# Hybrid mLSTM and windowed-attention layer: TensorE in a fixed order through the attention, value products of two steps together, gate chain and v weights placed anew

## The chip, the cores and the metric

The kernel runs on one core of one Trainium2 chip. The metric is the time of one execution on the device, in microseconds (us). TensorE (PE in the profile) multiplies matrices into PSUM, VectorE (DVE) and ScalarE (ACT) evacuate PSUM and do the elementwise work, GpSimd (POOL) does elementwise work between SBUF tiles, and SyncE (SP) issues the DMAs. Each engine works through its own queue in order, and semaphores join them.

## The reference

One layer of a bidirectional encoder on 1024 tokens of width 1024, in float32. A single input projection feeds two groups of heads:

- four mLSTM heads of width 128: q and k go through a centred convolution of five taps and a SiLU; input and forget gates give a chunkwise recurrence with a matrix state, once forward and once backward; the two directions are added, normalised per head and gated by a sigmoid of the projection o;
- eight attention heads of width 64 with two key/value heads: each block of 128 queries sees its own block of keys and the two beside it, with a distance penalty and a sink logit per head.

Both results go through the output projection, then `x <- LN(alpha*x + mix)`, then a SwiGLU FFN of inner width 2816 with a gated per-layer input, and a second layer norm.

```python
s = jnp.einsum('bnqhgd,bnkhd->bnhgqk', qb, kb) * (A_HEAD_DIM ** -0.5)
s = jnp.where(valid[:, None, None], s + bias, -jnp.inf)
mx = jnp.maximum(s.max(-1, keepdims=True), sk)
e = jnp.exp(s - mx)
prob = e / (e.sum(-1, keepdims=True) + jnp.exp(sk - mx))
out = jnp.einsum('bnhgqk,bnkhd->bnqhgd', prob, vb)
```

## The kernel before, in words

**Precision.** Most matrices are kept as a pair: a rounded high part and the low rest (`split`, L90: ScalarE casts the high part, POOL or DVE subtracts). `mm3` (L111) multiplies two such pairs with three products, high by high, high by low, low by high; one call of it over a contraction of 128 is what the text calls a projection unit, with a moving operand of 512 columns. Transposes, value products and the mLSTM products are plain float32; a float32 product is two records in the trace.

**Order.** The program is traced in the order in which the code is written, and a planner then orders each engine's queue: it simulates the engines and takes, at each moment, the ready instruction that was traced first. Long projections are "fillers" (L119 to L174): generators that yield after each unit. `fill(n)` (L125) traces the next n units at a lower priority, so that they go where TensorE has nothing better; `until(name)` forces a tile to be finished. The planner may set any instruction earlier or later than its place in the text as long as its data allow it.

**Stages of the core.**

1. *First projection* (L293 to L315): attention keys and values and the gates of all 1024 tokens, eight PSUM banks c0ps; ScalarE copies the keys to akn (L314), DVE copies the values to av and adds the gate biases.
2. *Keys* (L324 to L335): per half of the tokens four transposes into one bank, 128 columns of two key heads each; then each head's 64 rows are copied to both the upper and the lower 64 partitions of k2, high part on ScalarE and low part on DVE.
3. *Gate chain* (L337 to L412): the prelude (L343 to L349) makes log-sigmoids on DVE and ScalarE; then TensorE transposes (gt), DVE scans (L359 to L363), two small products (gmp, mcp), and a last set of transposes (gcp) that DVE copies to gcol. Two results go to DRAM (mwd) for later.
4. *v weights* (L420 to L424): four loads of 512 KB on SP into the two-buffered raw tile, which the aq and qk weights also use, each split into vuh (ScalarE) and vul (POOL).
5. *Attention* (L501 to L514): 32 steps (four pairs of heads by eight query blocks). Step i traces `scores` (L446: four products, then softmax on DVE and ScalarE, last scaled by POOL at L467), then `transposed` of step i - 2 (L470: four or six transposes; ScalarE evacuates the first half of eT, DVE the second), then `weighted` of step i - 3 (L484: value products, each with 64 columns of the array, into one bank per four steps). Between them stand `fill(1)`, `fill(3)` and `fill(1)` (RA, L29). The fillers there are the aq tiles (queries), the eight v tiles and the first two qk tiles, 160 units in the loop.
6. *mLSTM heads* (L544 to L638): per head transposes of k, state products `up` (L568) in six groups, score products, numerators `nd` (L607, L609), normalisation of hs (L625), and for the head before it `gated` (L628): transposes tr of hs, multiplied into the sigmoid of o. Fillers: qk tiles 2 to 7, o tiles, and the attention part of the output projection. A qk tile ends in five passes of convolution over 1024 columns on DVE (L282, L284).
7. Output projection, first layer norm, FFN with Winograd-style sums, second layer norm; the change does not touch them.

Of the kernel before, what the change touches and what calls it, by code (L numbers as in the profile page):

```python
# [7 lines left out]
F32 = mybir.dt.float32  # L8
# [20 lines left out]
RA = (1, 3, 1)  # L29
# [6 lines left out]
def hybrid_layer(  # L36
# [7 lines left out]
    pe, act, dve, pool = nc.tensor, nc.scalar, nc.vector, nc.gpsimd  # L44
# [54 lines left out]
    def load_w(src, shape, name, eng_lo=None, raw=None):  # L99
        if raw is None:  # L100
            raw = wp.tile([P] + shape, F32, name="raw_" + name, tag="raw", bufs=2)
        nc.sync.dma_start(raw, src)
        hi = wp.tile([P] + shape, F32R, name="hi_" + name, tag="whi", bufs=4)
        lo = wp.tile([P] + shape, F32R, name="lo_" + name, tag="wlo", bufs=4)
        f = flat if len(shape) == 2 else (lambda t: t)
        split(f(hi), f(lo), f(raw), eng_lo)
        return hi, lo
# [200 lines left out]
    akn = [Y([P, 4, P], F32, f"akn{i}") for i in range(2)]  # L308
    GI = W([P, 2, MH, NT], F32, "GI")
    GF = W([P, 2, MH, NT], F32, "GF")  # L310
    for t in range(NT):
        dve.tensor_tensor(GI.rearrange("p d h c -> p (d h) c")[:, :, t], c0ps[t][:, 256:264], bg[:, 0:8], ALU.add)
        dve.tensor_tensor(GF.rearrange("p d h c -> p (d h) c")[:, :, t], c0ps[t][:, 264:272], bg[:, 8:16], ALU.add)
        act.copy(akn[t // 4][:, t % 4, :], c0ps[t][:, 0:128])  # L314
        dve.tensor_copy(av[:, t, :], c0ps[t][:, 128:256])  # L315

# [7 lines left out]
    for hf in range(2):  # L324
        akT = bank(f"akT{hf}", "sp")
        for t in range(4):
            pe.transpose(akT[:, t * P:(t + 1) * P], akn[hf][:, t, :], ident)
        cs = slice(hf * 512, hf * 512 + 512)
        for kv in range(2):
            src = akT[kv * 64:kv * 64 + 64, :]  # L330
            h, l = k2[kv]
            act.copy(h[0:64, cs], src)
            act.copy(h[64:128, cs], src)
            dve.tensor_tensor(l[0:64, cs], src, h[0:64, cs].bitcast(F32), ALU.subtract)
            dve.tensor_tensor(l[64:128, cs], src, h[64:128, cs].bitcast(F32), ALU.subtract)  # L335
# [14 lines left out]
    gt = bank("gt", "et")  # L350
    pe.transpose(gt[:G64, 0:P], g3, ident)
    pe.transpose(gt[:G64, P:2 * P], gi, ident)
    lfI = gA[:G64, 192:448].rearrange("p (a b) -> p a b", b=P)
    dve.tensor_copy(lfI.rearrange("p a b -> p (a b)"), gt[:G64, 0:2 * P])
    bt = gA[:G64, 448:576]
    Ar = gA[:G64, 576:704]
    Mr = gA[:G64, 704:832]
    gm = gA[:G64, 832:834]
    dve.tensor_tensor_scan(bt[0:32, :], ones[0:32, :], lfI[0:32, 0, :], 0.0, ALU.mult, ALU.add)  # L359
    dve.tensor_tensor_scan(bt[32:64, ::-1], ones[32:64, :], lfI[32:64, 0, ::-1], 0.0, ALU.mult, ALU.add)  # L360
    dve.tensor_tensor(Ar, lfI[:, 1, :], bt, ALU.subtract)
    dve.tensor_tensor_scan(Mr[0:32, :], Ar[0:32, :], Ar[0:32, :], -BIG, ALU.max, ALU.max)
    dve.tensor_tensor_scan(Mr[32:64, ::-1], Ar[32:64, ::-1], Ar[32:64, ::-1], -BIG, ALU.max, ALU.max)  # L363
    dve.tensor_copy(gm[0:32, 0:1], bt[0:32, P - 1:P])
    dve.tensor_copy(gm[32:64, 0:1], bt[32:64, 0:1])
    dve.tensor_copy(gm[0:32, 1:2], Mr[0:32, P - 1:P])
    dve.tensor_copy(gm[32:64, 1:2], Mr[32:64, 0:1])
    gmp = bank("gmp", "et")
    pe.matmul(gmp[0:1, 0:64], gm[:, 0:1], ident[:64, :64], start=True, stop=True)
    pe.matmul(gmp[0:1, 64:128], gm[:, 1:2], ident[:64, :64], start=True, stop=True)  # L370
    ext = gB[0:1, 0:144].rearrange("p (a b c) -> p a b c", a=2, b=8)
    dve.memset(ext[:, 0, :, 0:1], -BIG)
    dve.memset(ext[:, 1, :, 0:1], BIG)
    for q in range(2):
        v = gmp[0:1, q * 64:q * 64 + 64].rearrange("p (s c) -> p s c", c=8)
        dve.tensor_copy(ext[:, q, 0:4, 1:9], v[:, 0:4, :])
        dve.tensor_copy(ext[:, q, 4:8, 1:9], v[:, 4:8, ::-1])
    mrow = gB[0:1, 144:216].rearrange("p (a b) -> p a b", b=9)
    dve.tensor_tensor_scan(
        mrow.rearrange("p a b -> p (a b)"), ext[:, 1].rearrange("p a b -> p (a b)"),  # L380
        ext[:, 0].rearrange("p a b -> p (a b)"), 0.0, ALU.max, ALU.add)
    m64 = gB[0:1, 216:280].rearrange("p (a b) -> p a b", b=8)
    dve.tensor_copy(m64[:, 0:4, :], mrow[:, 0:4, 0:8])
    dve.tensor_copy(m64[:, 4:8, ::-1], mrow[:, 4:8, 0:8])
    mcp = bank("mcp", "et")
    pe.matmul(mcp[0:64, 0:1], m64.rearrange("p a b -> p (a b)"), one_c[0:1, 0:1], start=True, stop=True)
    mc = gB[:G64, 280:284]
    dve.tensor_copy(mc[:, 0:1], mcp[0:64, 0:1])
    dve.tensor_tensor(mc[:, 1:2], mc[:, 0:1], gm[:, 1:2], ALU.max)
    dve.tensor_scalar(mc[:, 2:3], mc[:, 1:2], -1.0, None, ALU.mult)  # L390

    mwr = gB[:G64, 288:544].rearrange("p (a b) -> p a b", b=P)
    Mt = mwr[:, 0, :]
    dve.tensor_scalar(Mt, Mr, mc[:, 0:1], None, ALU.max)
    act.activation(mwr[:, 1, :], Mt, AF.Exp, bias=mc[:, 0:1], scale=-1.0)
    mwd = dr.tile([2, MH, NT, 2, P], F32, name="mwd")
# [290 lines left out]
    for h in range(MH):  # L687
        mlstm_head(h)
        if h:
            gated(h - 1)  # L690
# [603 lines left out]
```

## Time and profile before

| what | value |
|---|---|
| median of 3 runs | 1270.44 us (1269.13 to 1271.46) |
| the profiled execution | 1267.67 us |
| its span, first to last instruction | 1265.9 us |
| PE busy | 1223.8 us, 97% |
| PE weight loads (PEld) | 1011.4 us, 80% |
| DVE busy | 848.8 us, 67% |
| ACT busy | 520.0 us, 41% |
| POOL busy | 395.2 us, 31% |
| granted TensorE clock, mean | 0.989 |

Busy time is the union of an engine's instructions. TensorE's products overlap: one of 512 columns is recorded as some 0.39 us long, while the next starts sooner, so what a product takes from the queue is the distance between starts. A share of the whole span is a mean over stages: what one stage is worth is read from that stage. [...]

### The profile page before, as it was taken

The page shows a single profiled execution, that of the slowest core. Times are in us where ns is not written, and L with a number is a line of the kernel's source. Part 1 is how long each engine was busy: PE and PEld are TensorE (multiplying, and loading weights), DVE is VectorE, ACT ScalarE, POOL GpSimd, SP SyncE. Part 2 cuts the span into 40 slices and gives each one's busy share as a digit, 9 for nine tenths or more (in the row PEclk, how much of TensorE's full clock was granted, in tenths as well). Part 3 has the DMA queues.
Part 4 walks back from the last instruction along what each step waited for, and adds up shares of the span by engine and source line. Part 5 has one row for each costly group of instructions (what it writes and reads, how often), then busy time and mean ns, then how long its engine had stood idle before and what let it go on. Part 6 is the DMA issues. An engine that isn't in the chain of part 4 may idle for free.

```text
span 1265.9 us, 16488 instructions
## 1 busy us (share of the span) xinstructions
PE 1223.8 (97%) x6009; PEld 1011.4 (80%) x6009; DVE 848.8 (67%) x1549; ACT 520.0 (41%) x928; POOL 395.2 (31%) x297
## 2 busy tenths in 40 slices
PE   8899999999899998799999999999999999999996
PEld 8777777788788877678888888888887888888885
DVE  6656546677878679665766676767558696564666
ACT  5545444555465124543433433333334343333332
POOL 5522223333354025322332332233227541000007
PEclk9999999999999999899999999999999999999998
DMA  7311111511247122104645455546326646666603
GB/s 244 117 36 61 41 59 42 171 34 67 83 142 278 64 100 102 64 26 166 217 149 208 144 197 175 185 165 224 107 93 216 236 161 220 198 196 195 192 1 133
DMA packets 68785, 174.40 MB, mean 138 GB/s; under 512 B 7328, under 2 KB 12128, under 8 KB 68704
## 3 DMA queue, kind: packets, MB, share of 16 engines
q1 hardware_dynamic: 68704, 173.35, 40.2%
q8 instruction: 47, 0.77, 0.3%
q14 instruction: 34, 0.28, 0.1%
HBM read 126.86 MB, written 46.47 MB: 137 GB/s over the span
## 4 chain that ended last, share of the span: by engine, by line
PE 85%; DVE 7%; DMA 2%; ACT 2%; POOL 2%; issue 2%; POOLq 0%; SPq 0%; DVEq 0%; ACTq 0%
PE ma L113 6%; PE ma L112 6%; PE ma L114 6%; PE mc L113 3%; PE mc L114 3%; PE mc L112 3%; PE op L492 2%; PE oa L113 2%; PE oa L112 2%; PE oa L114 2%; PE ob L113 2%; PE ob L112 2%; PE ob L114 2%; PE yo L112 2%; PE yo L114 2%; PE yo L113 2%
## 5 line engine op out<-in xcount | busy, mean ns | idle before, releaser
L897 POOL TENSOR_TENSOR s<-ru,rg 128x512 f32<-128x512 f32 x22 | 29.5, 1343 | 187.1 <-DMA ru<-in_wffi_dram 185.3
L467 POOL TENSOR_SCALAR e<-e,st 128x384 f32<-128x384 f32 (+1 forms) x64 | 36.1, 577 | 119.3 <-DVE st L465 96.1
L1210 POOL TENSOR_TENSOR rs<-rs,mhalf 128x1 f32<-128x1 f32 x8 | 9.4, 1184 | 182.8 <-DVE rs L1209 182.7
L965 DVE TENSOR_TENSOR us<-us,ma 128x512 f32<-128x512 f32 x22 | 15.1, 684 | 64.6 <-PE ma L114 64.6
L463 ACT ACTIVATE e<-e,st 128x384 f32<-128x384 f32 (+1 forms) x64 | 37.2, 582 | 39.7 <-DVE st L459 39.5
L112 PE MATMUL yo<-hi_wo,mh 128*128 128x512 f32 x128 | 50.7, 396 | 1.1 <-DVE y L663 1.1
L112 PE MATMUL pj_qk<-xh,hi_qk 128*128 128x512 f32 x128 | 50.9, 398 | 0.0
L113 PE MATMUL pj_qk<-xl,hi_qk 128*128 128x512 f32 x128 | 50.9, 398 | 0.0
L114 PE MATMUL pj_qk<-xh,lo_qk 128*128 128x512 f32 x128 | 50.6, 395 | 0.0
L91 ACT CAST a4h<-s 128x512 fp32r<-128x512 f32 x22 | 13.7, 621 | 89.7 <-POOL s L897 42.5
L113 PE MATMUL yo<-lo_wo,mh 128*128 128x512 f32 x128 | 50.3, 394 | 0.0
L114 PE MATMUL yo<-hi_wo,ml 128*128 128x512 f32 x128 | 49.8, 393 | 0.0
L906 POOL TENSOR_TENSOR s<-ru 128x512 f32<-128x512 f32 x22 | 37.4, 1701 | 39.2 <-DVE a2l L97 39.2
L457 DVE CUSTOM_DVE_ANT_0 e<-sp,bias 128x384 f32<-128x384 f32 (+1 forms) x64 | 32.3, 522 | 24.5 <-PE sp L456 23.3
L91 ACT CAST a2h<-s 128x512 fp32r<-128x512 f32 x44 | 26.2, 620 | 52.4 <-PE mc L113 36.6
L902 POOL TENSOR_TENSOR s<-rg,s 128x512 f32<-128x512 f32 x22 | 28.7, 1303 | 58.4 <-DVE a4l L97 58.4
L284 DVE SCALAR_TENSOR_TENSOR qk<-pre,colt,qk 128x1024 f32<-128x1024 f32 x32 | 45.8, 1432 | 0.4
L112 PE MATMUL mb<-b21h,a1h 128*128 128x512 f32 x88 | 35.0, 398 | 2.4 <-ACT b21h L748 2.4
L874 DVE TENSOR_TENSOR sa<-sb,sa 128x512 f32<-128x512 f32 x11 | 8.3, 752 | 43.3 <-DMA sb<-in_wffo_dram 43.3
L960 DVE TENSOR_TENSOR yb<-yb,us 128x512 f32<-128x512 f32 x22 | 37.0, 1683 | 0.3 <-ACT yb L959 0.3
L112 PE MATMUL ma<-t2h,a2h 128*128 128x512 f32 x88 | 34.6, 394 | 1.3 <-ACT a2h L91 0.7
L898 POOL TENSOR_TENSOR s<-s,ru 128x512 f32<-128x512 f32 x22 | 32.6, 1484 | 9.8 <-DVE a3l L97 8.2
(901 smaller groups left out, 4203.6 us busy)
## 6 DMA issues: line engine op xcount, KB each, us to landing
fb<-hb SPq DMA_DIRECT2D x35, 512.0 KB, 4.5
rg<-in_wffi_dram SPq DMA_DIRECT2D x22, 512.0 KB, 3.6
ru<-in_wffi_dram SPq DMA_DIRECT2D x22, 512.0 KB, 5.2
fa<-sb SPq DMA_DIRECT2D x20, 512.0 KB, 3.5
mw<-mwd SPq DMA_DIRECT2D x16, 512.0 KB, 5.4
fa<-in_wffo_dram SPq DMA_DIRECT2D x15, 512.0 KB, 3.8
hb<-ya SPq DMA_DIRECT2D x11, 512.0 KB, 3.8
hb<-yc SPq DMA_DIRECT2D x11, 512.0 KB, 2.9
```

Source lines behind the costliest of these rows:

```text
L91: act.copy(dst_hi, src)
L112: pe.matmul(o, ah, bh, start=start, stop=False, skip_group_check=goes_on)
L113: pe.matmul(o, ah, bl, start=False, stop=False, skip_group_check=goes_on)
L114: last["mm"] = pe.matmul(o, al, bh, start=False, stop=stop, skip_group_check=goes_on)
L284: dve.scalar_tensor_tensor(y, pre[:, w:w + S], colt[:, ct, w:w + 1], y, ALU.mult, ALU.add)
L457: dve.tensor_tensor_reduce(e[:, i, :L], sp[:, :L], biasd[j][:, i, off:off + L], 1.0, -BIG, ALU.add, ALU.max, accum_out=st[:, i:i + 1])
L463: act.activation(e[:, i, :L], e[:, i, :L], AF.Exp, bias=st[:, i:i + 1], accum_out=st[:, 2 + i:3 + i])
L467: pool.tensor_scalar(e[:, i, :L], e[:, i, :L], st[:, 6 + i:7 + i], 0.0, ALU.mult, ALU.add)
L897: pool.tensor_tensor(s3, ru[:, lo, :], rg[:, lo, :], ALU.subtract)
L898: pool.tensor_tensor(s2, s3, ru[:, up, :], ALU.add)
L906: pool.tensor_tensor(s1, ru[:, lo, :], ru[:, up, :], ALU.add)
L960: dve.tensor_tensor(hb_, hb_, u, ALU.mult)
```

## The change

- A wrapper around TensorE's calls: while `strict[0]` is true, each product or transpose is pinned in issue order behind the one traced before it. It is true from the end of the first projection to the end of the attention loop. The pin is an order in the queue, not a wait.
- The loop: `weighted` is called for two steps at once, on even steps; eT has three buffers; `RA` is (1, 2, 1), so 135 filler units are traced in the loop.
- Keys: akn holds each head's 64 columns twice, so that a transpose gives both copies; 16 transposes into four banks in place of eight into two, and 128-partition evacuations, four on each engine in place of eight.
- The gate chain becomes a generator whose five parts are traced between units and steps; its prelude is traced ahead of the keys. In the order of the text: 4 units, keys, 4 units, gt, 8 units, the loop; gmp in step 1, mcp in step 2, gcp in step 4.
- v weights: the raw buffers of loads 1 to 3 first get one column from the last key tile (DVE), so that the load follows the keys; POOL's low part is done in two halves, there and in every weight load that names no engine.
- Heads: `gated` transposes are queued behind the second `up` group of the next head, and for the last head behind the last projection product traced, with four units ahead of it.

```diff
-RA = (1, 3, 1)
+RA = (1, 2, 1)
...
+    strict = [False]
+
+    class pe:
...
+        def put(ins):
+            return tc.keep_in_program_order(ins) if strict[0] else ins
...
-        split(f(hi), f(lo), f(raw), eng_lo)
+        split(flat(hi), flat(lo), flat(raw), eng_lo or "halves")
...
-    akn = [Y([P, 4, P], F32, f"akn{i}") for i in range(2)]
+    akn = [Y([P, 4, 2, P], F32, f"akn{i}") for i in range(2)]
...
-        act.copy(akn[t // 4][:, t % 4, :], c0ps[t][:, 0:128])
+        act.copy(akn[t // 4][:, t % 4].rearrange("p k (u d) -> p k u d", u=2),
+                 c0ps[t][:, 0:128].rearrange("p (k d) -> p k d", k=2).unsqueeze(2).to_broadcast([P, 2, 2, 64]))
...
+    strict[0] = True
+    fill(4)
...
-    for hf in range(2):
-        akT = bank(f"akT{hf}", "sp")
-        for t in range(4):
-            pe.transpose(akT[:, t * P:(t + 1) * P], akn[hf][:, t, :], ident)
-        cs = slice(hf * 512, hf * 512 + 512)
-        for kv in range(2):
-            src = akT[kv * 64:kv * 64 + 64, :]
-            h, l = k2[kv]
-            act.copy(h[0:64, cs], src)
-            act.copy(h[64:128, cs], src)
-            dve.tensor_tensor(l[0:64, cs], src, h[0:64, cs].bitcast(F32), ALU.subtract)
-            dve.tensor_tensor(l[64:128, cs], src, h[64:128, cs].bitcast(F32), ALU.subtract)
+    def keys():
+        for hf in range(2):
+            cs = slice(hf * 512, hf * 512 + 512)
+            for kv in range(2):
+                akT = bank(f"akT{hf}{kv}", ("sp", "et")[hf])
+                for t in range(4):
+                    pe.transpose(akT[:, t * P:(t + 1) * P], akn[hf][:, t, kv, :], ident)
+                h, l = k2[kv]
+                act.copy(h[:, cs], akT)
+                dve.tensor_tensor(l[:, cs], akT, h[:, cs].bitcast(F32), ALU.subtract)
...
+    def gates():
+        gt = bank("gt", "op")
+        pe.transpose(gt[:G64, 0:P], g3, ident)
...
+        yield
+        gmp = bank("gmp", "et")
...
+        yield
+        mcp = bank("mcp", "et")
...
+        yield
+        gcp = bank("gcp", "et")
...
+    keys()
+    fill(4)
+    chain = gates()
+    next(chain)
+    fill(8)
...
         raw = wp.tile([P, 2, 512], F32, name=f"vraw{kp}", tag="raw", bufs=2)
+        if kp:
+            dve.tensor_copy(raw[:, 0, 0:1], k2[1][1][:, S - 1:S].bitcast(F32))
         nc.sync.dma_start(raw, wv[kp])
...
-        split(flat(vu[kp][0]), flat(vu[kp][1]), flat(raw))
+        split(flat(vu[kp][0]), flat(vu[kp][1]), flat(raw), "halves")
...
-        eT = W([P, 2, 384], F32, "eT", 2)
+        eT = W([P, 2, 384], F32, "eT", 3)
...
-    drain(1)
...
         if 2 <= i < len(steps) + 2:
+            if i == 2:
+                fill(4)
             transposed(*steps[i - 2])
             fill(RA[1])
-        if i >= 3:
+        if i >= 4 and i % 2 == 0:
+            weighted(*steps[i - 4])
             weighted(*steps[i - 3])
-            fill(RA[2])
+        if i in (1, 2, 4):
+            next(chain)
+        fill(RA[2])
+    strict[0] = False
...
-    def gated(h):
+    def gated(h, after):
...
+            with tc.issue_after(after.ins):
+                for cc in range(4):
+                    pe.transpose(tr[:, cc * P:(cc + 1) * P], hs[:, cc, :], ident)
...
-            gated(h - 1)
+            gated(h - 1, last["up", 0])
...
-    gated(MH - 1)
+    fill(4)
+    gated(MH - 1, last["mm"])
```

## Rows read from the trace of the kernel before

**Rows 1.** Stretches: length, busy us of PE, PEld, DVE, ACT, POOL, clock, DMA, GB/s.

```profile
48.90:60.00 11.10, 7.81 (x30) 6.37 (x31) 9.42 (x18) 6.09 (x11) 5.27 (x4) 0.85 0.48 138
...
101.00:145.00 44.00, 44.00 (x283) 33.72 (x282) 25.81 (x93) 20.90 (x66) 11.41 (x19) 1.00 0.14 49
...
300.00:380.00 80.00, 73.51 (x413) 62.53 (x412) 65.72 (x174) 43.47 (x81) 36.88 (x27) 0.98 0.35 110
```

**Rows 2.** Timeline of PE, 101.4 to 106 us: start, us, instruction.

```profile
101.41 0.40 PE L113 MATMUL pn_v<-vul,xh 128*128 128x512 f32 x1
101.73 0.88 PE L492 MATMUL op<-eT,av 128*64 128x128 f32 x12
102.54 0.38 PE L455 MATMUL sp<-k2h,q 128*128 128x256 f32 x1
...
102.89 0.49 PE L477 MATMUL et<-ident,e 128*128 128x128 f32 x3
103.31 0.43 PE L492 MATMUL op<-eT,av 128*64 128x128 f32 x2
103.67 0.50 PE L114 MATMUL pn_v<-vuh,xl 128*128 128x512 f32 x1
...
104.43 0.87 PE L492 MATMUL op<-eT,av 128*64 128x128 f32 x10
105.23 0.44 PE L455 MATMUL sp<-k2h,q 128*128 128x384 f32 x1
105.51 0.34 PE L456 MATMUL sp<-k2l,q 128*128 128x384 f32 x1
105.69 0.39 PE L112 MATMUL pn_v<-vuh,xh 128*128 128x512 f32 x1
105.91 0.39 PE L113 MATMUL pn_v<-vul,xh 128*128 128x512 f32 x1
```

**Rows 3.** Timeline of PE, a group of 8 value records and its successor.

```profile
121.15 0.66 PE L492 MATMUL op<-eT,av 128*64 128x128 f32 x8
121.74 0.50 PE L113 MATMUL pj_aq<-xl,hi_aq 128*128 128x512 f32 x1
```

**Rows 4.** Timeline of PE, first and last group of value records.

```profile
76.49 0.43 PE L492 MATMUL op<-eT,av 128*64 128x128 f32 x2
...
236.56 0.65 PE L492 MATMUL op<-eT,av 128*64 128x128 f32 x6
```

**Rows 5.** Timeline of all engines at the end of the gates' prelude.

```profile
48.42 2.34 POOL L97 TENSOR_TENSOR lo_aq<-raw_aq,hi_aq 128x1024 fp32r<-128x1024 f32 x1 [0.37 <-ACT hi_aq L91]
48.82 1.99 DVE L345 TENSOR_SCALAR gA<-gA 128x64 f32<-128x64 f32 x1
...
53.76 0.23 DVE L349 TENSOR_TENSOR gA<-gA 128x64 f32<-128x64 f32 x1 [0.26 <-ACT gA L347]
```

**Rows 6.** Timeline of PE, the first product behind the first projection.

```profile
30.58 0.39 PE L112 MATMUL pj_aq<-xh,hi_aq 128*128 128x512 f32 x1
```

**Rows 7.** The page's costliest groups, convolution on DVE: count, busy us, mean ns.

```profile
L284 DVE SCALAR_TENSOR_TENSOR qk<-pre,colt,qk 128x1024 f32<-128x1024 f32 x32 | 45.8, 1432 | 0.4
```

**Rows 8.** Timeline of PE, head 1's second state group and head 0's first transpose.

```profile
299.00 0.83 PE L568 MATMUL up<-va,ks 128*128 128x129 f32 x6
...
315.37 0.27 PE L635 MATMUL tr<-ident,hs 128*128 128x128 f32 x1
```

**Rows 9.** Waits of PE: total us, times, longest.

```profile
PE tr L635 <- DVE hs L625: 5.4, 4, 1.8
```

**Rows 10.** Timeline, two steps: last score product and POOL's scaling of the weights.

```profile
166.43 0.34 PE L456 MATMUL sp<-k2l,q 128*128 128x384 f32 x1
...
170.01 1.15 POOL L467 TENSOR_SCALAR e<-e,st 128x384 f32<-128x384 f32 x2 [2.78 <-DVE st L465]
...
217.21 0.28 PE L456 MATMUL sp<-k2l,q 128*128 128x256 f32 x1
...
227.34 0.93 POOL L467 TENSOR_SCALAR e<-e,st 128x256 f32<-128x256 f32 x2 [6.68 <-DVE st L465]
```

More of the change, by code (lines that the diff above doesn't have):

```diff
@@ L43, in hybrid_layer, with matmul, transpose @@
     nc = tc.nc
-    pe, act, dve, pool = nc.tensor, nc.scalar, nc.vector, nc.gpsimd
+    act, dve, pool = nc.scalar, nc.vector, nc.gpsimd
+    strict = [False]
+    class pe:
+        @staticmethod
+        def put(ins):
+            return tc.keep_in_program_order(ins) if strict[0] else ins
+        @staticmethod
+        def matmul(*args, **kw):
+            return pe.put(nc.tensor.matmul(*args, **kw))
+        @staticmethod
+        def transpose(*args, **kw):
+            return pe.put(nc.tensor.transpose(*args, **kw))
     const = ctx.enter_context(tc.tile_pool(name="const", bufs=1))
@@ L104, in load_w @@
         lo = wp.tile([P] + shape, F32R, name="lo_" + name, tag="wlo", bufs=4)
-        f = flat if len(shape) == 2 else (lambda t: t)
-        split(f(hi), f(lo), f(raw), eng_lo)
+        split(flat(hi), flat(lo), flat(raw), eng_lo or "halves")
         return hi, lo
@@ L349, in hybrid_layer @@
     dve.tensor_tensor(g3, g3, g2, ALU.subtract)
[L350 to L395, printed above, removed]
-    mwd = dr.tile([2, MH, NT, 2, P], F32, name="mwd")
-    nc.sync.dma_start(mwd.rearrange("d h c q t -> (d h c) q t"), mwr)
@@ L398, in hybrid_layer @@
-    rows = gB[:G64, 544:800].rearrange("p (a b) -> p a b", b=P)
-    act.activation(rows[:, 0, :], Ar, AF.Exp, bias=mc[:, 2:3])
-    dve.tensor_tensor(bt, bt, Mt, ALU.add)
-    act.activation(rows[:, 1, :], bt, AF.Exp, scale=-1.0)
-    act.activation(mc[:, 3:4], mc[:, 1:2], AF.Exp, bias=mc[:, 0:1], scale=-1.0)
-    gcp = bank("gcp", "et")
-    pe.transpose(gcp[:, 0:64], Ar, ident[:64, :64])
-    for q in range(2):
-        pe.transpose(gcp[:, 64 * (q + 1):64 * (q + 2)], rows[:, q, :], ident[:64, :64])
@@ L407, in hybrid_layer @@
-    pe.matmul(gcp[:, 192:256], mc[:, 3:4].to_broadcast([G64, P]), ident[:64, :64], start=True, stop=True)
-    gcol = const.tile([P, 4, 64], F32, name="gcol")
-    dve.tensor_copy(gcol.rearrange("p a b -> p (a b)"), gcp[:, 0:256])
-    kscale = float(P) ** -0.5
-    dve.tensor_scalar(gcol[:, 1, :], gcol[:, 1, :], kscale, None, ALU.mult)
-    cA, cWA, cFL, cDE = (gcol[:, i, :] for i in range(4))
+    gcol = const.tile([P, 4, 64], F32, name="gcol")
+    kscale = float(P) ** -0.5
+    cA, cWA, cFL, cDE = (gcol[:, i, :] for i in range(4))
@@ L567, in mlstm_head @@
                     c = order[idx]
-                    pe.matmul(up[:, i * 129:i * 129 + 129], ks[d, c // 4][:, c % 4, :], va_[:, c, :], start=True, stop=True)
+                    last["up", g] = pe.matmul(up[:, i * 129:i * 129 + 129], ks[d, c // 4][:, c % 4, :], va_[:, c, :], start=True, stop=True)
                 for i, idx in enumerate(idxs):
@@ L633, in gated @@
             tr = bank("tr", "ma")
-            for cc in range(4):
-                pe.transpose(tr[:, cc * P:(cc + 1) * P], hs[:, cc, :], ident)
+            with tc.issue_after(after.ins):
+                for cc in range(4):
+                    pe.transpose(tr[:, cc * P:(cc + 1) * P], hs[:, cc, :], ident)
             ss = so[:, hf * 512:hf * 512 + 512]
```

54 lines of the change are left out of this document (added).

## The prediction

> **What bounds the kernel now.** I read four views: the page, the busy time by stretch, TensorE's own timeline in the attention, and the waits. The page's busy shares (in the table above) show TensorE (PE) at work for 97% of the span and VectorE (DVE) for 67%. The stretches [rows 1] say where that is literal: from 101 to 145 us, inside the attention, PE is busy for all 44.00 us at full clock, with DVE at 25.8, so a nanosecond taken from PE's queue there comes off the end. Two other stretches are not full. [...]
>
> "Busy" hides a second cost. In PE's timeline [rows 2] the distance from one start to the next is what an instruction really takes. A group of value products (L492, 64 columns of the array wide) disturbs its neighbours. The projection product before it takes 0.32 us (101.41 to 101.73) where an undisturbed one takes 0.22 (105.69 to 105.91): +0.10. The score product behind it takes 0.28 (105.23 to 105.51) where the same shape takes 0.18 (105.51 to 105.69): +0.10. Inside, 12 records take 0.81 and 8 records 0.59 [rows 2, 3], so two pairs cost 0.22, one pair 0.11, and six pairs would be 0.66: another +0.15. One visit to this form thus costs 0.10 + 0.10 + 0.15 = 0.35 us over its work. Often the planner makes two visits for one step: the first product goes as soon as ScalarE's half of the transposed block is there (2 records, 0.36, 103.31 to 103.67), the other 10 records later (0.80, from 104.43). That is 1.16 against 0.66, so +0.50, and twice 0.20 at the borders: 0.90 us. Between the first and the last such group [rows 4] there are 51: 19 of 2 records, 15 of 10, 9 of 12, 4 of 6 and 4 of 8. So 19 of the 32 steps are split and 13 are whole.
>
> **The sum, part by part.**
>
> *Value products of two steps together, pinned.* Now 19 x 0.90 + 13 x 0.35 = 21.7 us. After: 16 visits of 20 or 24 records, 16 x 0.35 = 5.6 us. That is **-16.1 us**, all on PE, which is full there. Nothing has to be late for this; it is PE's own time.
>
> *Keys transposed in both copies at once.* Eight more transposes. Three of them took 0.42 before a value group, of which 0.10 is that group's [rows 2], so 0.11 each: **+0.9 us** on PE. ScalarE and DVE each make four 128-partition evacuations in place of eight 64-partition ones, before the first scores; the key copies out of the projection become twice as wide. Both lie beside projection units.
>
> *The start.* The stretch 48.9 to 60 lost 3.3 us standing and 0.15 x 11.1 = 1.7 us of clock, 5.0 together [rows 1]. The stand came because q's evacuation was late on DVE. There DVE was behind: the gate chain's tiny L345 took 1.99 us, and the prelude ended only at 53.99 [rows 5]. In the new program text the prelude stands ahead of the key evacuations, and three of four v weight loads wait for the keys, so neither sits in front of them on ScalarE or GpSimd (POOL). The pinned order puts 4 units of projection (12 products of 0.22, 2.6 us) ahead of the 16 key transposes (1.8), 4 between these and the gate transposes, 8 (5.3) before the first scores. The first projection ends at 30.6 [rows 6], so the gate transposes come 7.0 us later, at 37.6; the prelude, unobstructed, is seven short instructions and one table load. I take the 5.0 us back and charge 1.0 us for new short waits: **-4.0 us** (bounds -5.0, and +13 in the second rival).
>
> Where a wait is added: each late v load sits at the head of SP's queue until DVE has written one column of its buffer, and behind it stand the other v loads and the aq weights. Their first user, the first v tile, is the 33rd projection unit, about 15 us after the first scores, so this costs 0; with that cover gone it costs the last split, 2.34 us [rows 5], and the load ahead of it. The DVE copies also wait for buffers that POOL frees, and the first softmax stands behind them. POOL's lo halves in two pieces are the same work; a DVE instruction held up behind one waits half as long. L345's 1.99 us ran inside POOL's 2.34 us split [rows 5].
> [...]
>
> *Fewer projection units in the loop.* Three per step become two behind the transposes, so 135 units run inside instead of 160. The work is the same and is done later: nine units of the second qk tile fall behind the loop, and head 0 must then wait for them and for DVE's convolution (four passes of 1.43 us and a first one [rows 7], some 7 us). PE has the 32 units of qk tiles 2 and 3 (21 us) to do meanwhile: 0 us. With that cover gone, 5.9 + 7 = 13 us.
>
> *Output-gate transposes pinned behind the next head's second state product.* That order holds already: the second group of head 1 starts at 299.00, head 0's first transposes at 315.37 [rows 8]. The waits they have today, 5.4 us in four [rows 9], come from a late DVE, which the edit does not change. The four units and the pin for the last head likewise only fix an order. 0 us; from the 6.5 us idle and 1.6 us of clock at 300 to 380 [rows 1] the bounds are -8 and +8, the upper one as an equal loss if the planner's new order of this stage is the worse one. *eT in three buffers, class for PE:* no work of their own.
>
> Sum: -16.1 + 0.9 - 4.0 = **-19.2 us**. The profiled execution took 1267.7 us (span 1265.9 and 1.8 around it) and would take 1248.5; the median of the runs shown is 2.8 above it, so I predict 1270.4 - 19.2 = **1251.2**.
>
> **The rivals.**
>
> *The two steps still pay twice* (they write different columns of the bank, so there may be a border between them). For: no group of more than 12 records is in the trace. Against: inside a group, pairs of different keys follow at 0.11 with no border [rows 2, 3]. Then 32 x 0.35 = 11.2 remain instead of 5.6: 1256.8.
>
> *The gate chain holds up the pinned order.* Now PE does other work while the chain runs; pinned, it must stand. If the prelude ended as late as now (53.99, [rows 5]) PE would stand from 37.6 to 54 us, +16 us, and lose another 1.7 us to the clock. The old stand is gone: 1270.4 - 16.1 + 0.9 - 5.0 + 16 + 1.7 = 1267.9. For: DVE's slow start. Against: the prelude's earlier place in the text.
>
> *Slower: every step waits for its softmax.* Two steps now take 2 x (0.72 + 0.66) + 8 x 0.66 + 12 x 0.11 + 0.35 = 9.7 us (four score products, six transposes, the units, the value products). From the end of a step's scores to its transposes that leaves about 10.4 us (those 9.7 and one unit). One step needed 4.4 us from scores to scaled weights (166.77 to 171.16), one beside the convolution 10.8 (217.49 to 228.27) [rows 10]. From 10.4 on, PE stands, since the pinned order lets nothing pass. If each step took 12, two steps would take 1.6 us longer, 32 steps 26 us: 1277. Against: DVE is busy 59% in this stage [rows 1], and the convolution now falls at the loop's end.
> [...]
>
> *The heads get quicker too*: shorter POOL pieces before a late DVE take back the 8.1 us of idle and clock at 300 to 380 [rows 1]: 1243.
>
> **How the numbers follow.** Forecast 0.64, quicker heads 0.13, border between steps 0.07, gate chain 0.10, softmax 0.06. The range runs from 1240 (quicker heads, start all taken back) to 1264 (the heads' +8 and half a gate stand); it leaves out most of the last two cases. 0.2% is 2.5 us, about what a measurement of this kernel can tell from no change. Faster: the first three and 0.04 of the gate chain, 0.88; same: 0.05, from the gate chain; slower: 0.07, the softmax case and the worst of the gate chain.
>
> **What would show it.** Right: 16 groups of 20 to 24 value records, each some 1.25 to 1.5 us from start to start; PE full from 31 us to the heads; the last value products near 201 us (236.6 [rows 4], less 25 units of 0.66 moved behind them, less the sum). Wrong: PE waits at the gate transposes or at score or weight transposes in the attention; groups split again; more idle PE at the heads than 6.5 us in 80.

## The result, and the profile after

| | before | after |
|---|---|---|
| median | 1270.11 us (1269.13 to 1271.46, 4 runs) | 1253.45 us (1253.33 to 1253.83, 4 runs) |
| profiled execution, span | 1267.67, 1265.9 us | 1253.4, 1251.6 us |
| PE, DVE, ACT, POOL busy | 1223.8, 848.8, 520.0, 395.2 us | 1211.1, 848.6, 512.3, 397.6 us |
| granted clock, mean | 0.989 | 0.988 |

The ratio is 0.9869 [0.9851, 0.9886], 16.7 us faster; 1251.2 was predicted. The work of the other three engines is nearly the same, so the gain is not work taken from them: it is TensorE's own time and its stands. (After the change all products stand under L56 and all transposes under L60, the wrapper's lines, so they are told by tile.)

The value products, PE's timeline of the kernel after. They answer to [rows 2 to 4]:

```profile
64.55 1.31 PE L56 MATMUL op<-eT,av 128*64 128x128 f32 x20
...
103.64 0.40 PE L56 MATMUL pn_v<-vuh,xl 128*128 128x512 f32 x1
103.97 1.31 PE L56 MATMUL op<-eT,av 128*64 128x128 f32 x20
105.22 0.50 PE L56 MATMUL pn_v<-vuh,xh 128*128 128x512 f32 x1
105.56 0.40 PE L56 MATMUL pn_v<-vul,xh 128*128 128x512 f32 x1
...
206.97 1.09 PE L56 MATMUL op<-eT,av 128*64 128x128 f32 x14
208.65 0.65 PE L56 MATMUL op<-eT,av 128*64 128x128 f32 x6
```

The product ahead of the group takes 0.33 from start to start, 0.10 over its 0.23. The 20 records take 1.25, where ten pairs at 0.11 would take 1.10. The first product behind takes 0.34, again some 0.10 more. That is one visit at 0.35, as in [rows 2]; nothing more is paid between the two steps. There are 17 groups where there were 51; only the last pair, at the loop's end, is broken in two (14 and 6).

The stretches of the kernel after (columns as in [rows 1]):

```profile
31.60:49.00 17.40, 17.40 (x93) 14.22 (x91) 13.43 (x45) 11.19 (x21) 6.15 (x5) 1.00 0.26 92
49.00:60.00 11.00, 11.00 (x56) 9.09 (x56) 9.46 (x34) 8.36 (x23) 9.43 (x11) 1.00 0.29 96
101.00:145.00 44.00, 44.00 (x303) 36.56 (x302) 26.27 (x91) 21.89 (x65) 15.54 (x24) 1.00 0.15 55
300.00:380.00 80.00, 73.83 (x418) 62.78 (x417) 64.58 (x172) 41.75 (x82) 33.19 (x25) 0.98 0.54 180
```

The stretch that had 7.81 of 11.10 us at a clock of 0.85 [rows 1] is full at 1.00. In 44 us of full attention PE now gets 303 records done instead of 283. In the heads the stretch looks as it did, 73.83 of 80 us at 0.98, though it no longer holds the same work; the count below shows that the stands there grew.

How the start comes out, timeline of all engines of the kernel after, to be held against [rows 5]:

```profile
34.34 1.91 PE L60 MATMUL akT<-ident,akn 128*128 128x128 f32 x16
34.53 0.23 DVE L367 TENSOR_TENSOR gA<-gA 128x64 f32<-128x64 f32 x1 [0.85 <-ACT gA L365]
...
38.85 0.27 PE L60 MATMUL gt<-ident,gA 128*64 128x128 f32 x1
```

The prelude's last step, which stood at 53.76, is at 34.53, four us ahead of the gate transposes that need it.

PE's waits in the kernel after, from the end of the attention to the end of the heads (total, times, longest). tr are the transposes of hs, pp a head's score products, which wait here for DVE's scaling of the keys (ks), yo the output projection:

```profile
PE tr L60 <- DVE hs L662: 4.5, 3, 1.9
PE pp L56 <- DVE ks L593: 2.5, 2, 1.4
PE yo L56 <- DVE y L701: 1.2, 2, 0.8
PE nd L56 <- DVE hs L654: 0.9, 1, 0.9
PE up L56 <- DVE C L611: 0.7, 1, 0.7
...
```

The first row answers to [rows 9] (5.4 in four). The second is new: before the change PE did not wait at pp. In the attention itself only one wait is left, 0.2 us of a v product for a bank.

**Where the time went.** I added up PE's distances from start to start, from the last product of the first projection to the last one of the output projection. "Stand" is what distances over 0.45 us have beyond 0.23. "Half" is the time at a granted clock of 0.50 (1.00 is full), which costs half of it: in the kernel before, products of 512 columns start 0.43 us apart where the clock is 0.50 (54.15 to 54.58; 0.50 over 54 to 56) and 0.23 apart where it is 1.00 (57.30 to 57.53; 1.00 over 57 to 60). "Switch" is what value groups and their neighbours take beyond 0.055 us per record and the neighbours' undisturbed distances.

| profile of | length | stand | half | switch | rest |
|---|---|---|---|---|---|
| before | 470.1 | 15.1 | 6.8 | 20.9 | 430.6 |
| after | 452.2 | 12.5 | 3.4 | 5.9 | 432.1 |
| one step at a time | 458.0 | 12.5 | 6.8 | 11.6 | 430.6 |
| not pinned | 472.3 | 13.1 | 10.2 | 24.0 | 430.1 |
| four steps | 450.1 | 13.0 | 6.8 | 2.4 | 431.3 |
| gate chain at once | 463.7 | 22.4 | 13.7 | 6.1 | 428.4 |
| two, then four | 449.9 | 13.1 | 6.8 | 2.6 | 430.9 |
| three units | 459.6 | 14.9 | 17.1 | 6.2 | 430.0 |
| keys as before | 456.2 | 16.4 | 6.8 | 5.9 | 430.4 |

Before to after: switch -15.0, stand -2.6, clock -1.7, rest +1.5, together -17.9 with the rounding. The stands up to the last value product fell from 5.0 us (1.1, 3.3 and 0.5) to 0.3, those behind it rose from 10.2 to 12.2. Outside this stretch the profile of after is 3.6 us longer: 1.0 ahead of it and 2.6 behind. Both vary with the execution. No edit touches these parts, except that weight splits come in halves. The first projection ended between 30.4 and 31.6 us in the fourteen profiles, and the part behind took 765.3 to 768.9, short where the second stretch at half clock behind the first norm lasted 3.4 us, and long where it lasted 6.8 or more. The executions of one kernel (the one without the gated pin, below) differ likewise, from 1249.7 us at a mean clock of 0.990 to 1254.3 at 0.987. So -17.9 is the profile's measure of the change, and -16.7 that of the medians.

### The profile page after: what moved, and what is told of

It is laid out like the page before. It is cut to its first block, busy times and chain, and to the rows that moved or that the text cites. A ratio compares the mean times of both kernels' runs of the same rounds, so it can differ in the third digit from the quotient of the medians.

```text
span 1251.6 us, 16503 instructions
## 1 busy us (share of the span) xinstructions
PE 1211.1 (97%) x6017; PEld 1007.8 (81%) x6017; DVE 848.6 (68%) x1548; ACT 512.3 (41%) x920; POOL 397.6 (32%) x317
## 4 chain that ended last, share of the span: by engine, by line
PE 84%; DVE 7%; DMA 3%; ACT 2%; issue 2%; POOL 2%; SPq 0%; POOLq 0%; ACTq 0%; DVEq 0%
PE ma L56 19%; PE mc L56 9%; PE oa L56 7%; PE ob L56 7%; PE yo L56 6%; PE pj_qk L56 5%; PE mb L56 5%; PE pg L56 4%; PE pj_aq L56 4%; PE pn_v L56 4%; PE pj_o L56 2%; PE op L56 2%; PE sp L56 2%; PE nd L56 1%; PE et L60 1%
## 5 line engine op out<-in xcount | busy, mean ns | idle before, releaser
L1004 DVE TENSOR_TENSOR us<-us,ma 128x512 f32<-128x512 f32 x22 | 15.1, 685 | 63.3 <-PE ma L56 63.3
L56 PE MATMUL yo<-hi_wo,mh 128*128 128x512 f32 x128 | 51.5, 402 | 1.7 <-DVE y L701 1.2
L299 DVE SCALAR_TENSOR_TENSOR qk<-pre,colt,qk 128x1024 f32<-128x1024 f32 x32 | 51.5, 1608 | 0.6
L56 PE MATMUL pj_qk<-xh,hi_qk 128*128 128x512 f32 x128 | 51.4, 402 | 0.0
L107 ACT CAST a4h<-s 128x512 fp32r<-128x512 f32 x22 | 13.7, 621 | 90.5 <-PE ma L56 46.2
L56 PE MATMUL pj_qk<-xl,hi_qk 128*128 128x512 f32 x128 | 50.7, 396 | 0.0
L56 PE MATMUL pj_qk<-xh,lo_qk 128*128 128x512 f32 x128 | 50.6, 395 | 0.0
L56 PE MATMUL yo<-lo_wo,mh 128*128 128x512 f32 x128 | 50.4, 394 | 0.0
L56 PE MATMUL yo<-hi_wo,ml 128*128 128x512 f32 x128 | 49.7, 392 | 0.0
L56 PE MATMUL mb<-b21h,a1h 128*128 128x512 f32 x88 | 35.1, 398 | 2.6 <-ACT b21h L787 2.6
L511 ACT COPY eT<-et 128x384 f32<-128x384 f32 (+1 forms) x32 | 14.4, 450 | 54.5 <-PE et L60 54.4
```

Source lines behind the costliest of these rows:

```text
L56: return pe.put(nc.tensor.matmul(*args, **kw))
L107: act.copy(dst_hi, src)
L299: dve.scalar_tensor_tensor(y, pre[:, w:w + S], colt[:, ct, w:w + 1], y, ALU.mult, ALU.add)
L1004: (eng or dve).tensor_tensor(dst, x, y_, ALU.add)
```

## The experiments

Each kernel is the changed one with one edit, and each ratio is to the kernel before on the same chip. The changed kernel itself has 0.9869.

**One step at a time.**

```diff
-        if i >= 4 and i % 2 == 0:
-            weighted(*steps[i - 4])
+        if i >= 3:
             weighted(*steps[i - 3])
```

> The changed kernel with one edit undone: value products go one step at a time again (32 visits of 8 or 12 records instead of 17 groups of up to 24), still pinned. My theory (a visit of TensorE to the 64-column form costs 0.35 us beside its work): 16 visits more, +5.6 us, about 1259.0 us. Rival (the pinned order and the new start made the gain, a visit has no price of its own): 1253.5 us, within 1 us.

1257.61 us, 0.9911 [0.9898, 0.9925]. The groups, PE's timeline:

```profile
105.17 0.40 PE L56 MATMUL pn_v<-vuh,xl 128*128 128x512 f32 x1
105.50 0.88 PE L56 MATMUL op<-eT,av 128*64 128x128 f32 x12
106.30 0.50 PE L56 MATMUL pn_v<-vuh,xh 128*128 128x512 f32 x1
```

Each step but the last is a whole visit of its own, 33 in all; switching costs 5.7 us more than after, 16 visits more at 0.36. In the medians it is 5.3 (0.0042 of 1270), where 5.6 was expected. That is the worth of the pairs alone, and the price of a visit.

**Not pinned.**

```diff
-    strict[0] = True
+    strict[0] = False
```

> The changed kernel without the pins: the planner orders TensorE in the attention as it did before, all else as changed, value products of two steps still traced side by side. My theory: the planner sends the first product of a group ahead of the others again, 40 to 51 groups, +10 to +15 us in the attention; the good start stays since it comes from the order of the text: 1262 to 1268 us. Rival (the pairing in the text is enough, the pins are idle): 16 to 20 groups, 1253 to 1255 us.

1272.72 us, 1.0028 [1.0018, 1.0037]: slower than before the change, and above the 1262 to 1268 that I expected. PE's timeline over five microseconds:

```profile
99.77 0.43 PE L56 MATMUL op<-eT,av 128*64 128x128 f32 x2
...
103.09 0.66 PE L56 MATMUL op<-eT,av 128*64 128x128 f32 x8
103.68 0.44 PE L56 MATMUL sp<-k2h,q 128*128 128x384 f32 x1
...
104.79 0.44 PE L56 MATMUL op<-eT,av 128*64 128x128 f32 x4
```

The calls for two steps are in the text, but the planner again issues each product as its half of eT comes: 56 groups, switching at 24.0 us. All the other edits without the pin are worth nothing in sum. What the pairs gain, they gain by the fixed order. The start is another matter: it stays good without the pin, as expected. PE is busy for all of 31.6 to 49 us, and its waits from there to the end of the attention are one row, a stand at 70 us:

```profile
PE et L60 <- ACT eT L511: 2.0, 1, 2.0
```

**Four steps together.** The value products of four steps at every fourth step, ahead of that step's transposes; eT in four buffers. To make room, the output copy osb is two tiles with two DMAs, and the constants of ones and the gate tiles lie in the gates' scratch tiles.

```diff
+        if i >= 6 and (i - 2) % 4 == 0:
+            for k in range(i - 6, i - 2):
+                weighted(*steps[k])
...
-        if i >= 4 and i % 2 == 0:
-            weighted(*steps[i - 4])
-            weighted(*steps[i - 3])
```

> The changed kernel with the value products of four steps together, ahead of the transposes, with four eT buffers; to make room the attention result is stored from two half-size tiles with two DMAs, and gate inputs and the ones row lie in the gate tiles. My theory: 8 visits instead of 17 groups, 9 x 0.35 = -3 us, about 1250.5 us. Rival (larger groups make the evacuation or the next scores late, TensorE waits at the bank or at scores): no gain, 1253 to 1256 us.

1250.85 us, 0.9855 [0.9842, 0.9869]. Eight groups of 44, PE's timeline:

```profile
71.36 0.56 PE L56 MATMUL pn_v<-vuh,xh 128*128 128x512 f32 x1 [2.15 <-DVE q L281]
...
75.21 2.62 PE L56 MATMUL op<-eT,av 128*64 128x128 f32 x44
77.76 0.87 PE L60 MATMUL et<-ident,e 128*128 128x128 f32 x6
```

Forty-four records take 2.55 us, 0.13 over 22 pairs at 0.11: the price inside belongs to the visit, not to the step. Switching falls by 3.5 us more. Part of that is given back in the first row: with no value products early in the loop a v product comes before DVE has emptied its bank, PE stands 2.15 us and then works 3.4 us at half clock (the next products of 512 columns start 0.43 us apart, 71.72 to 72.15). The time is what I expected (1250.5), but the interval overlaps that of the changed kernel, so the medians alone do not settle the gain.

**Two, then four.** The kernel of four steps, with two together in the first two groups.

```diff
-        if i >= 6 and (i - 2) % 4 == 0:
+        if i >= 10 and (i - 2) % 4 == 0:
...
+        if i in (4, 6):
+            weighted(*steps[i - 4])
+            weighted(*steps[i - 3])
```

> Value products of four steps together, but of two in the first four steps. With four everywhere 1250.85 us (0.9855) and a new stand of 2.15 us at 68.8 us (a v product waits for the bank of the last q tile, whose evacuation DVE had late), and half clock for 3.4 us after it. My theory: two groups of about 1.3 us that come earlier, ahead of that place, cover the stand; switching costs one more visit (0.35): -2.15 -1.7 +0.35 = -3.5: 1247 to 1248.5, ratio 0.983. Rival (what is late is DVE, and each value group only moves the wait to the next bank): the stand is there in another place, 1250.5 to 1252.

1248.7 us (1247.79 to 1250.99), 0.9837 [0.9824, 0.9851], the best of the study. PE's waits in the attention, the only row:

```profile
PE pn_v L56 <- DVE q L281: 1.4, 1, 1.4
```

The stand shrank instead of going, and the stretch at half clock behind it is gone; the time is just above what I expected. In this execution the heads had 3.4 us more at half clock, so the table's column has 6.8 in both kernels. The interval touches those of the changed kernel and of four steps, so the step from these is likely and not settled.

**The gate chain at once.** All five parts run ahead of the loop.

```diff
     chain = gates()
-    next(chain)
+    for _ in chain:
+        pass
...
-        if i in (1, 2, 4):
-            next(chain)
```

> The changed kernel with all five parts of the gate chain traced at the first part's place, so the pinned products gt, gmp, mcp and gcp stand one behind the other. My theory: TensorE stands there while DVE and ScalarE work, about 3.5 us before gmp, 2 before mcp and 3 before gcp, plus up to 1.7 us of clock behind it: +8 to +11 us, 1261 to 1264 us. Rival (the chain's place is of no weight because TensorE gets the time back later): 1253 to 1255 us.

1264.91 us, 0.9969 [0.9958, 0.9979]. PE's timeline, the waits at the chain:

```profile
41.20 0.27 PE L56 MATMUL gmp<-ident,gA 64*1 64x64 f32 x2 [2.77 <-DVE gA L389]
43.06 0.27 PE L56 MATMUL gmp<-ident,gA 64*1 64x64 f32 x2 [1.60 <-DVE gA L391]
46.50 0.34 PE L56 MATMUL mcp<-one_c,gB 1*64 1x1 f32 x2 [3.16 <-DVE gB L409]
48.47 0.56 PE L60 MATMUL gcp<-ident,gB 64*128 64x64 f32 x2 [1.34 <-ACT gB L424]
```

This is the rival in which the gate chain holds up the pinned order, made on purpose: four stands, 8.9 us, and 10.2 us at half clock (the mean is 0.83 from 31.6 to 49 us and 0.91 from 49 to 75). Of the 16.7 us 12.7 are lost again (0.0100 of 1270). I expected 1261 to 1264: the stands are about what I had, the clock costs 5.1 instead of 1.7. Spreading the chain over the steps is what makes the pin affordable.

**The gate prelude behind the keys.** The seven instructions of the prelude are traced behind `keys()` and four units.

```diff
-    dve.scalar_tensor_tensor(g1, gf, -1.0, gf, ALU.mult, ALU.max)
...
     keys()
     fill(4)
+    dve.scalar_tensor_tensor(g1, gf, -1.0, gf, ALU.mult, ALU.max)
...
     chain = gates()
```

> The changed kernel (0.9869 of before) with the gate prelude traced behind the keys and the four units, where the kernel before had it behind the key evacuations. My theory (the prelude's place ahead of the keys is what takes the start's stand away): DVE and ScalarE do the key evacuations and the table load first, g3 is ready 2 to 4 us later than 34.8 us, after the place of the gate transposes (38.85 us in the changed kernel) or near it: TensorE stands up to 3 us at gt, with up to 1.7 us of clock: 1254 to 1258, ratio 0.987 to 0.990. Rival 1 (the fixed order alone does it, since key and gate work is short once nothing else is in front): no stand at gt, 1253 to 1254. Rival 2 (late g3 as before the change, 54 us): a stand of over 10 us, 1265 or more.

1254.16 us, 0.9884 [0.987, 0.9899], no difference that can be measured. PE's timeline at the gate transposes:

```profile
39.29 0.30 PE L60 MATMUL gt<-ident,gA 128*64 128x128 f32 x1 [0.36 <-DVE gA L439]
```

The prelude ends 4.5 us later, and PE stands 0.36 us. That lies between my theory's lower end and rival 1, nearer to the rival: the prelude's place is not what takes the stand away.

**v weights as before, POOL in one piece.**

```diff
-        split(flat(hi), flat(lo), flat(raw), eng_lo or "halves")
+        split(flat(hi), flat(lo), flat(raw), eng_lo)
...
         if kp:
-            dve.tensor_copy(raw[:, 0, 0:1], k2[1][1][:, S - 1:S].bitcast(F32))
+            pass
...
-        split(flat(vu[kp][0]), flat(vu[kp][1]), flat(raw), "halves")
+        split(flat(vu[kp][0]), flat(vu[kp][1]), flat(raw))
```

> The changed kernel (1253.4 us, 0.9869 of before) with the v weights as before: no column from the key tile ahead of the loads, and GpSimd's low parts in one piece everywhere. My theory: the start was cured by the prelude's place and the fixed order, and both of these edits cost and give nothing there (the forecast's 0 us): 1252 to 1255, ratio to before 0.986 to 0.988, TensorE's stands between the first projection and 60 us within 1 us of the changed kernel's. Rival 1 (the late loads are the cure): the 2.3 us splits are again among the prelude and the key evacuations, TensorE stands at the gate or weight transposes for 3 to 6 us and loses 2 to 5 us of clock: 1258 to 1264. [...]

1255.8 us (1253.09 to 1258.94), 0.9889 [0.9873, 0.9905]: some 2.5 us worse by the medians, 0.8 above my theory's range, and the interval overlaps that of the changed kernel, so it is not settled. DVE's timeline, the long rows and a short one of the same line; then PE's waits in the attention:

```profile
42.54 1.54 DVE L383 TENSOR_TENSOR_SCAN gA<-ones,gA 32x128 f32<-32x128 f32 x1
45.97 2.16 DVE L386 TENSOR_TENSOR_SCAN gA<-gA 32x128 f32<-32x128 f32 x1
50.92 0.16 DVE L492 TENSOR_TENSOR st<-snk,st 128x2 f32<-128x2 f32 x1
54.69 2.32 DVE L492 TENSOR_TENSOR st<-snk,st 128x2 f32<-128x2 f32 x1
```

```profile
PE sp L56 <- DVE st L489: 1.8, 2, 1.5
PE et L60 <- POOL e L499: 0.6, 1, 0.6
```

The DVE instruction that took 0.16 us at 50.92 took 2.32 at 54.69, where a POOL split ran (54.60, 2.40 long), and 2.4 us of PE's stands follow. This execution was the slowest of its five, so the stands say what can happen rather than the mean.

**Keys as before.** Eight transposes, and each head's rows copied to both halves of the partitions.

```diff
-    akn = [Y([P, 4, 2, P], F32, f"akn{i}") for i in range(2)]
+    akn = [Y([P, 4, P], F32, f"akn{i}") for i in range(2)]
...
-                act.copy(h[:, cs], akT)
-                dve.tensor_tensor(l[:, cs], akT, h[:, cs].bitcast(F32), ALU.subtract)
+                act.copy(h[0:64, cs], src)
+                act.copy(h[64:128, cs], src)
+                dve.tensor_tensor(l[0:64, cs], src, h[0:64, cs].bitcast(F32), ALU.subtract)
+                dve.tensor_tensor(l[64:128, cs], src, h[64:128, cs].bitcast(F32), ALU.subtract)
```

> The changed kernel with the keys as before: eight transposes, each head's rows copied to both halves of the partitions by eight evacuations on ScalarE and eight on DVE. My theory (0.9 us of TensorE is all that the copies cost, and the evacuations are covered by eight units before the first scores): TensorE's eight transposes fewer give -0.9 us: 1252 to 1253.5, no stand at the first scores. Rival (the evacuations are on the path): eight more on each engine of about 0.5 to 0.6 us; keys are ready some 2 to 4 us later, gate transposes' copy and the v loads too: stands at gmp, sp or pn_v of 1 to 4 us: 1254 to 1258.

1256.09 us, 0.9897 [0.9882, 0.9912]: 3.6 us worse, though PE has less to do. PE's timeline, its stands in the attention:

```profile
45.37 0.35 PE L56 MATMUL sp<-k2h,q 128*128 128x256 f32 x1 [1.10 <-DVE q L281]
47.81 0.44 PE L56 MATMUL sp<-k2h,q 128*128 128x384 f32 x1 [0.60 <-DVE st L491]
56.61 0.89 PE L60 MATMUL et<-ident,e 128*128 128x128 f32 x4 [1.75 <-DVE st L498]
60.03 0.27 PE L56 MATMUL mcp<-one_c,gB 1*64 1x1 f32 x2 [1.14 <-ACT eT L513]
```

The rival has it, though the interval still touches that of the changed kernel; the stands are plain in the trace. Four evacuations more on each engine put q, the softmax and the chain behind, and the fixed order stands for each: 4.6 us, less 0.9 of transposes.

**Three units behind the transposes**, as before the change, and **fewer**: the last unit of a step only in every second one.

```diff
-RA = (1, 2, 1)
+RA = (1, 3, 1)
```

> The changed kernel with three units behind the transposes (1, 3, 1), as before the change: 160 or so units in the loop in place of 135. My theory: units cost the same wherever they stand, and what is behind the loop covers the convolution in both cases (the forecast's 0 us): 1252.5 to 1254.5. Rival 1 (the shorter loop left the heads 2.1 us worse): -1.5 to -2.5 us: 1251 to 1252. Rival 2 (the slack): if two steps of 9.7 us were near the softmax's time, longer steps remove hidden stands in the loop; the trace shows none over 0.2 us, so this gives under 0.5 us. Rival 3: the convolution inside the loop makes DVE late for q, key or weight copies and the pinned order stands for it: +2 to +7 us: 1255 to 1260.

```diff
-        fill(RA[2])
+        fill(RA[2] if i % 2 else 0)
```

> The changed kernel with the last unit of each step only in every second step: 17 or 18 units fewer in the loop. With 25 more (1, 3, 1) it was 6 us slower (1258.8), because TensorE stood late in the heads, where units were then missing. Theory 1 (in this order 1, 2, 1 is about enough; what is left of the heads' stands is waits that the planner does not foresee; the second qk tile and its convolution come later for head 0): 0 to +4 us: 1253 to 1258. Theory 2 (each unit kept back for the heads is worth 0.2 us as from 190 to 156): -2 to -4 us: 1249 to 1251.5. Theory 3 (the shorter steps, some 9 us for two, meet the softmax): stands at et in the loop, over +3 us.

With three: 1258.76 us, 0.9918 [0.9903, 0.9932], 6 us worse. With fewer: 1253.58, 0.9878 [0.9863, 0.9893], no difference. Counted in the traces, the units done by the last value product are 167.7 before, 156.3 after, 190.7 with three and 138.3 with fewer. The stretch 375 to 425 us, first of the kernel with three, then of the kernel after, and PE's waits in the heads with three:

```profile
375.00:425.00 50.00, 39.84 (x222) 35.52 (x221) 37.90 (x142) 14.78 (x42) 14.76 (x11) 0.86 0.31 106
```

```profile
375.00:425.00 50.00, 49.82 (x271) 41.98 (x270) 39.72 (x123) 13.62 (x32) 13.09 (x11) 1.00 0.33 112
```

```profile
PE nd L56 <- DVE hs L654: 5.6, 3, 3.5
PE up L56 <- DVE C L611: 4.6, 2, 3.6
PE tr L60 <- DVE hs L662: 3.5, 5, 1.5
```

In that stretch 54 units run after the change and 24 with three. None of my expectations held. My theory had no difference, and rival 1 a gain of some 2 us in the heads from the longer loop; it is a loss of 6, by the trace in the heads. Rival 3's range has the number, but not its place: PE does not wait in the attention at all. What the loop takes is missing in the heads, and most of the loss is the clock (17.1 us at half clock against 3.4; the profiled execution was the slowest of its four). The pinned loop alone uses up more units than the planner did before the change, and RA gives them back. Holding back still more brings nothing: theory 1.

**Output-gate transposes not pinned**, without the four units.

```diff
-            with tc.issue_after(after.ins):
+            if True:
...
-    fill(4)
     gated(MH - 1, last["mm"])
```

> The changed kernel without the pin of the output-gate transposes and without the four units ahead of the last head's. My theory: the pin is the cause of the heads' worse stand (12.5 us in all but 2.1 more in this stage than before; tr waits 4.5 us in three against 5.4 in four): without it the stage stands as before, -1 to -2 us: 1251 to 1253. Rival 1 (the order holds already, 0 us, the forecast): 1253 to 1254.5 with the same waits at tr. Rival 2 (the pin helps, the stage is worse because the loop leaves nine more units of a qk tile to it): 1255 to 1260, more tr waits than 4.5 us.

1251.16 us (1249.67 to 1254.29), 0.9857 [0.984, 0.9874]. The time lies in my theory's range, but its cause is not there: the waits at tr are 4.5 us in three, as with the pin (rival 1); the order was there already. The medians differ by no more than their intervals: no cost and no gain is shown.

**qk tiles ahead of the last v tiles**, on the kernel of two, then four.

```diff
-    fillers += [v_tile(0), v_tile(1), aq_tile(2), v_tile(2), v_tile(3), aq_tile(3)] + [v_tile(t) for t in range(4, NT)]
-    fillers += [qk_tile(0), qk_tile(1)]
+    fillers += [v_tile(0), v_tile(1), aq_tile(2), v_tile(2), v_tile(3), aq_tile(3)] + [v_tile(4), v_tile(5), qk_tile(0), qk_tile(1), v_tile(6), v_tile(7)]
...
     strict[0] = False
+    fill(9)
```

> The best kernel so far (two steps in the first two groups, then four: 1248.7 us, 0.9837) with the first two qk tiles ahead of the last two v tiles, so that their convolution (7 us each on DVE) is over before the heads, and nine units traced behind the loop so that the last v tile is there. My theory: the two waits of TensorE for DVE's scaled keys at the heads' start (2.1 us) go, the pinned loop bears the convolution (with three units behind the transposes it bore it without a stand): -1 to -2.5 us: 1246 to 1248. Rival 1: DVE's convolution in the loop delays softmax or copies, TensorE stands in the loop, which lets nothing pass: +1 to +5 us. Rival 2: the units of the last v tiles are missing later, or the nine units behind the loop change the heads' order: 1248 to 1252.

1249.62 us, 0.9853 [0.9833, 0.9874], against 0.9837: no gain, where I expected 1 to 2.5 us. The waits at pp (2.1 us) are gone, and PE's waits in the attention have a new row:

```profile
PE et L60 <- ACT eT L511: 2.3, 1, 2.3
PE pn_v L56 <- DVE q L281: 1.3, 1, 1.3
```

What the heads gained, the fixed order lost elsewhere (PE's waits in the heads 2.4 us less, in the attention 2.2 more): rival 1.

## Why the prediction was right

*Switching, -16.1.* It measured -15.0 in the profile (20.9 to 5.9). The price of a visit held: 0.36 with single steps. One thing in it I had only for the split steps: a group with an odd number of pairs (2, 6, 10 or 14 records) pays 0.45, 0.25 of it inside, in every kernel, and one with an even number 0.35 (0.30 with 44 records). So 51 visits cost 20.9 before, and 56 cost 24.0 without the pin. Why the odd pair costs more stays open. The rival of a border between the two steps fell; four steps together cost one visit too. What the prediction left implicit is that the pairs bring this by the pin alone: without it there are 56 groups.

*The start, -4.0.* It measured -6.4: 4.7 of stand (5.0 to 0.3) and 1.7 of clock. The prediction read 3.3 us of stand from its stretch and left out 1.1 that ended at its edge, at 48.9, and 0.5 at 69.8; the 1.0 charged for new waits was not paid. And the reason was only half right. I put it first on the prelude's place ahead of the keys, and moving the prelude back cost nothing measurable. Nor does it need the pin: without it PE does not stand before 70 us either. What holds in that order is shorter work in front of each pinned product: the spread chain (12.7 us), the wide key evacuations (3.6), perhaps POOL's halves (2.5). No run takes all of them out at once, so what each did for the start stays open.

*Keys, +0.9.* This is a mis-sized term. The transposes cost what they were said to, 16 in 1.7 us, but "both lie beside projection units" is true only of the new form. In the pinned order the old evacuations cost 4.6 us of stands, so the edit is worth some -3.6 there. The sum did not suffer, since the start's term already reckoned with the new form and took no stand from the keys.

*Fewer units, 0.* Against the kernel before, the stands behind the loop are 2.0 us longer (10.2 to 12.2). The new row is pp <- DVE ks, 2.5 us in two at the first head: DVE's scaling of the keys comes behind passes of the convolution there, and the units at hand did not cover all of it. The row is not there before the change, nor with three units, nor with the qk tiles earlier. Against three units in the same order the edit gains 6 us. I costed the cover that the units behind the loop give ("the 32 units of qk tiles 2 and 3") as enough, and did not count how many the pinned loop would take from the heads. The same miscount gave the sign of 201 us for the last value products: by units it is 11 moved behind them, not 25, and they stand at 208.65.

*v loads, 0.* The three DVE copies took 0.29 for two and 0.15. POOL was idle beside the first two. The third ran beside a POOL half and was not lengthened, but DVE had stood 0.77 us until POOL freed its buffer, as the prediction said that it might; PE did not wait for it. DVE's timeline:

```profile
45.65 0.15 DVE L453 COPY vraw<-k2l 128x1 f32<-128x1 f32 x1 [0.77 <-POOL vul L111]
```

*Gated pin, 0.* Shown for the order (the same tr waits); for the time, within the intervals.

*The rivals.* The gate chain's mechanism is real and costs 12.7 us when its parts stand together. The softmax rival did not come: no wait at et or sp in the loop after the change, and with fewer units per step only 0.9 us at sp. Quicker heads did not come either: their stands grew.

*The sum.* Switching gave 1.1 us less than forecast and the start 2.4 more; the heads' stands, put at 0, took 2.0, and the rest 1.5 where 0.9 was charged for the keys. These misses partly cancel, so the main term is shown, and that -17.9 comes so near to -19.2 is in part luck.

## What to carry to other kernels

Count how often an engine at its limit changes the form of its work, and price the change from the distances between starts: here 0.35 or 0.45 us each, 51 times. A fixed order collects that gain, but it turns a late input into a stand of the whole engine (four of them, 8.9 us, with the gate chain at once), so each pinned instruction needs its inputs ready by the text: spread a serial chain over other work, and shorten what feeds it. Work that can go anywhere is a stock, to be kept for the stage where other engines are late, not spent where the engine is full anyway; beyond some point (here RA of 1, 2, 1) holding back more brought nothing.

## What was not expected of the hardware

Some small DVE instructions lasted nearly as long as the POOL split beside them: with the v weights as before, 2.16 us for a scan that takes 0.41 elsewhere and 2.32 for a small sum of 0.16, with POOL's splits at 2.40. With the splits in halves (1.29 each) the same sum took 1.22 in the kernel after, on DVE's timeline:

```profile
60.17 1.22 DVE L492 TENSOR_TENSOR st<-snk,st 128x2 f32<-128x2 f32 x1
```

How long a stand is does not tell by itself whether the clock falls behind it. One of 2.15 us was followed by 3.4 us at half clock (four steps together); one of 2.3 (qk tiles earlier), one of 1.4 (two, then four), one of 1.3 (qk tiles earlier) and one of 1.5 (v weights as before, 1.00 from 31.6 to 75 us) were followed by full clock. The two waits at pp are 2.5 us in three kernels alike. Behind them the clock was 1.00 after the change, 0.57 over four us with the prelude behind the keys, and 0.51 over seven with the output-gate transposes not pinned (columns as in [rows 1]):

```profile
237.20:247.00 9.80, 9.76 (x55) 8.49 (x56) 9.64 (x17) 3.07 (x4) 3.03 (x2) 1.00 0.28 89
...
238.60:242.60 4.00, 4.00 (x15) 3.48 (x16) 3.95 (x10) 1.53 (x2) 0.00 (x0) 0.57 0.26 102
...
237.00:244.00 7.00, 6.11 (x20) 5.33 (x21) 5.34 (x12) 2.54 (x4) 0.00 (x0) 0.51 0.25 75
```

So a stand that is taken away can pay more than its length, but how much differs, and differences of some us between two profiles can come from this alone.
